# Feed-forwards and output projections with the activations stationary, and a residual stream with tokens on partitions

## The chip, the cores and the metric

The kernel runs on one core of a Trainium2 chip. The metric is the device time of one execution in microseconds, the median over runs. All inputs are float32, the batch is one, and the sequence has 256 tokens. Only weights are packed and constants laid out on the host; the whole computation is one launch.

## The reference

The model is two layers of a decoder trunk, D = 2048. Layer 0 mixes with differential attention and an S5 state-space layer, layer 1 with RWKV-7. Around each mixer and each feed-forward stand two RMS norms, one before and one after:

```python
def _rmsnorm(x, gain, eps=1e-6):
    return x * lax.rsqrt(jnp.mean(x * x, axis=-1, keepdims=True) + eps) * gain

def _swiglu(h, w_gate, w_up, w_down):            # D_FF = 5632
    return (jax.nn.silu(h @ w_gate) * (h @ w_up)) @ w_down

for layer in range(2):
    gains = norm_gains[layer]
    h = _rmsnorm(x, gains[0])
    m = even_mixer(h) if layer == 0 else rwkv7_time_mix(h)   # each ends in "@ w_out" or "@ w_o", 2048 x 2048
    x = x + _rmsnorm(m, gains[1])
    f = _swiglu(_rmsnorm(x, gains[2]), w_gate[layer], w_up[layer], w_down[layer])
    x = x + _rmsnorm(f, gains[3])
```

In layer 1 the normed x of a token is mixed with that of the token before it, with six sets of weights per channel, ahead of the projections (receptances, keys, values, and three low-rank gates).

## The kernel before

**Layout.** Activations lie with channels on partitions: an array of 2048 channels and 256 tokens is sixteen tiles of 128 channels by 256 tokens. A norm's mean over channels is therefore a sum over partitions and tiles. Squares are summed tile by tile on GpSimd (`Acc`, line 464), and products with a column of 1/2048 on TensorE give a mean for each token (`rms_bc`, line 409). The power -1/2 is GpSimd's. Then `spread` (line 434) makes a diagonal of it and multiplies by ones, so that the value of each token stands on all partitions, for use as a tile of 128 by 256.

**Products.** For accuracy each operand is split into a rounded part and the rest, both float32r (`split`, line 390; for weights lines 317 and 318), and a product is three: high by high, high by low, low by high. In `mmb` (line 341) a 128x128 block of weights is stationary and 256 tokens move: three matmuls of 256 columns for each block. `n_outer` (line 351) runs over all k for one output tile of 128 channels; `k_steps` (line 372) holds several output tiles open and steps through k, so that TensorE can start when the first tiles of its input are there. `values` (line 1399) has it the other way already, for the values of both layers: 128 tokens of activations are stationary and four blocks side by side (512 columns) move, three matmuls for each half of the tokens.

**Weights.** All weight blocks lie in one stream in the order of use, eight to a chunk of 512 KB. `block` (line 321) takes the next; every eighth one calls `chunk_load` (line 308): a DMA on SyncE's queue, a rounding cast on ScalarE and a subtraction on VectorE, with three buffers for each of the three tiles, at a high priority.

**Order.** Instructions of an engine are ordered by a planner that simulates the program and takes priorities into account. `strict` keeps TensorE in the order in which the code is written. `warm` (line 295) issues products into a bank that nothing reads, while TensorE waits. PSUM's eight banks are three "pg", two "pa" and three "pb".

**The feed-forward** (`ffn`, line 1036). It first forms R of the mixer's norm. `post` (line 479) gives x += m R tile by tile, while the products of three tiles of gate and three of up follow in `k_steps` as x comes in. Each tile of x is split for the products with its gain as factor; the norm's R over x, which is known only at the end, is applied to the gate and up sums (lines 1070 and 1071). `pair` forms silu(gate) times up and splits it. Then `proj_out` (line 510) gives the down projection, its gain, its squares, and in layer 0 also the sums of x y and y y, so that `rms_two` (line 444) has R of the next layer's norm without a pass over the new x.

**The mixers' ends.** Layer 0's output projection is split: a first part (heads 0 to 4) fills waits of the mixer (`first`, line 744), and the rest is added to it (line 768). In layer 1 `wo` (line 1499) does it in four groups of heads: three of them as filler between the steps of the recurrence (`rwkv_values`), the last one by itself. `rwkv_keys` (line 1147) begins with x += m R0, h = x R1, the mix for the receptances and seven receptance tiles in `k_steps`.

**The end** (`forward`, line 1662): R of the last norm, `post`, and a store for every two tiles.

## Time and profile before

| | |
|---|---|
| median of three runs | 2703.03 us (2702.46 to 2706.29) |
| span of the profiled execution, first to last instruction | 2701.4 us |
| mean granted TensorE clock | 0.975 |
| read from and written to HBM | 448.02 MB, 27.79 MB |

The profiled execution's own time is given as its span alone; the nearest run is 1.1 us above it, the median 1.6.

| stretch, us from the span's start | what runs |
|---|---|
| 0 to 487 | layer 0's mixer, with its output projection at 428 to 487 |
| 487 to 535 | x += m R, first three tiles of gate and up |
| 535 to 1262.6 | feed-forward 0 |
| 1262.6 to 1329 | norm, mix, seven receptance tiles |
| 1329 to 1902 | layer 1's mixer; its last output projection group from 1877 |
| 1902 to 1955 | as at 487 |
| 1955 to 2681.7 | feed-forward 1 |
| 2681.7 to 2701.4 | last norm, sum and store |

A profile line of a group reads: line of the kernel, engine, operation, tile written <- tiles read, shapes, count | busy us, mean ns of one | idle time of the engine before them, and what ended it. A row of busy time by stretches gives the stretch, its length, busy time and instruction count of each engine, the granted clock, and DMA's share and rate. Matmuls are pipelined, so a matmul's own duration (its latency) is longer than the distance to the next; the distance is what a stream costs.

### The profile page before, as it was taken

Reading aid. Unit: us, or ns where it says so; the run is one execution under the profiler, and the core shown is the slowest. Engines: PE = TensorE matmul, PEld = TensorE weight load, DVE = VectorE, ACT = ScalarE, POOL = GpSimd, SP = SyncE. Lnnn points to the kernel's source line nnn. Section 1 sums busy time; section 2 is a strip of 40 time slices with the busy share of each in tenths; the row PEclk is TensorE's granted clock in tenths of the full one; section 3 lists DMA queues with packets and bytes.
Section 4 is the critical chain, followed back from the end, with each engine's and each line's share of the span. In section 5 each row is a group of like instructions: output and inputs, shape, how many; then the busy total and the mean of one; then the engine's idle time right before and its main releaser. Section 6 shows DMA issues by size and latency. Waiting matters only on the chain. (4 is left out here: it accounts for less than half of the span.)

```text
span 2701.4 us, 51244 instructions
## 1 busy us (share of the span) xinstructions
PE 2584.4 (96%) x20736; PEld 2459.2 (91%) x20736; DVE 1762.8 (65%) x2736; ACT 1180.7 (44%) x1847; POOL 585.0 (22%) x818
## 2 busy tenths in 40 slices
PE   8898899999999999998999889899899999999997
PEld 7775679899999999998899878799899999999997
DVE  7978875765556554445769979587766565554444
ACT  5332245544444444433766634353544444444342
POOL 4765622500000001113306530111600000000001
PEclk9999899999999999999999989899999999999999
DMA  6322235555555555555567687764455555555554
GB/s 218 110 102 86 86 125 181 175 186 184 183 183 185 181 191 199 193 181 186 171 209 239 208 220 207 179 198 158 173 187 185 181 187 180 186 181 184 183 182 162
DMA packets 218300, 479.14 MB, mean 177 GB/s; under 512 B 78672, under 2 KB 107600, under 8 KB 217040
## 3 DMA queue, kind: packets, MB, share of 16 engines
q1 hardware_dynamic: 218064, 475.88, 53.3%
q8 instruction: 162, 2.65, 0.4%
q14 instruction: 74, 0.61, 0.1%
HBM read 448.02 MB, written 27.79 MB: 176 GB/s over the span
## 5 line engine op out<-in xcount | busy, mean ns | idle before, releaser
L318 DVE TENSOR_TENSOR wl<-wr,wh 128x1024 fp32r<-128x1024 f32 x760 | 956.1, 1259 | 671.1 <-ACT wh L317 669.3
L317 ACT CAST wh<-wr 128x1024 fp32r<-128x1024 f32 x768 | 803.4, 1047 | 1156.1 <-PE pg L293 944.6
L293 PE MATMUL pg<-Z,wh 128*128 128x256 f32 x6368 | 1170.9, 286 | 18.5 <-ACT wh L317 11.0
L293 PEld LDWEIGHTS pg<-Z,wh 128*128 128x128 f32 x6368 | 1001.5, 194 | 39.7 <-issue 20.4
L293 PE MATMUL pg<-Z,wl 128*128 128x256 f32 x3184 | 905.5, 285 | 4.9 <-DVE wl L318 4.9
L293 PEld LDWEIGHTS pg<-Z,wl 128*128 128x128 f32 x3184 | 615.8, 194 | 6.5 <-DVE wl L318 6.4
L293 PE MATMUL pg<-PP,wh 128*128 128x256 f32 x2304 | 416.2, 283 | 0.0
L293 PEld LDWEIGHTS pg<-PP,wh 128*128 128x128 f32 x2304 | 359.4, 192 | 0.0
L293 PE MATMUL pg<-PP,wl 128*128 128x256 f32 x1152 | 326.0, 283 | 0.0
L293 PE MATMUL pg<-MX,wh 128*128 128x256 f32 x1408 | 271.4, 292 | 7.6 <-DVE MX L400 3.7
L475 POOL TENSOR_TENSOR n<-n,n 128x256 f32<-128x256 f32 x84 | 92.3, 1099 | 770.2 <-ACT n L473 768.3
L293 PEld LDWEIGHTS pg<-MX,wh 128*128 128x128 f32 x1408 | 224.7, 196 | 9.8 <-DVE MX L400 4.2
L293 PEld LDWEIGHTS pg<-PP,wl 128*128 128x128 f32 x1152 | 221.2, 192 | 0.0
L293 PE MATMUL pg<-MX,wl 128*128 128x256 f32 x704 | 201.7, 292 | 6.4 <-DVE wl L318 6.4
L293 PEld LDWEIGHTS pg<-MX,wl 128*128 128x128 f32 x704 | 136.9, 197 | 7.9 <-DVE wl L318 7.9
L544 POOL TENSOR_TENSOR ac<-f,M 128x256 f32<-128x256 f32 x1 | 0.7, 746 | 487.7 <-DVE M L542 487.7
L293 PE MATMUL pg<-X,wh 128*128 128x256 f32 x512 | 93.5, 283 | 0.0
L293 PE MATMUL pg<-wh,MX 128*128 128x512 f32 x256 | 90.0, 413 | 2.9 <-issue 2.6
L293 PEld LDWEIGHTS pg<-X,wh 128*128 128x128 f32 x512 | 79.9, 192 | 0.0
L293 PE MATMUL pg<-X,wl 128*128 128x256 f32 x256 | 72.4, 283 | 0.0
L1071 DVE TENSOR_TENSOR f<-pg,n 128x256 f32<-128x256 f32 x84 | 35.7, 425 | 52.2 <-PE pg L293 52.2
L293 PEld LDWEIGHTS pg<-wh,MX 128*128 128x128 f32 x256 | 49.7, 194 | 13.8 <-issue 3.0
(379 smaller groups left out, 3222.6 us busy)
## 6 DMA issues: line engine op xcount, KB each, us to landing
wr<-wst SPq DMA_DIRECT2D x776, 512.0 KB, 3.6
dr<-H SPq DMA_DIRECT2D x16, 512.0 KB, 4.2
CH<-dr SPq DMA_DIRECT2D x16, 512.0 KB, 4.7
dr<-X SPq DMA_DIRECT2D x12, 512.0 KB, 3.4
X<-dr SPq DMA_DIRECT2D x6, 1024.0 KB, 7.1
dr<-ak SPq DMA_DIRECT2D x16, 256.0 KB, 3.8
ln<-lnb SPq DMA_DIRECT2D x8, 512.0 KB, 4.4
S<-s5bc SPq DMA_DIRECT2D x4, 512.0 KB, 6.5
```

Source lines behind the costliest of these rows:

```text
L293: self.pe(self.nc.tensor.matmul(out, lhsT, rhs, start=start, stop=stop))
L317: nc.scalar.copy(h, r)
L318: (nc.gpsimd if pool else nc.vector).tensor_tensor(l, r, h.bitcast(F32), op=ALU.subtract)
L475: nc.gpsimd.tensor_tensor(self.cur[0], self.cur[0], sq, op=ALU.add)
L544: (v if last else gp).tensor_tensor(s[:, 1], xt, m[n], op=ALU.mult)
L1071: v.tensor_tensor(ur, u, Rh, op=ALU.mult)
```

## The change

Gate, up, down and both output projections take the form of `values`: 128 tokens stationary, 512 columns of weights moving. Their results, and x, m and the norms' sums, then have tokens on partitions: two arrays of 128 tokens by 2048 channels. R is a column per token half, used as a scalar for each partition; gains become rows that are loaded from DRAM. What goes into the next product must have channels on partitions, and is turned by transposes on TensorE (`flip`). The helpers `rms_bc`, `spread` and `Acc` stay in use for the first norm only; `post`, `proj_out` and `store_x` are gone.

The core of it (comments that the diff takes out, and lines of the same kind, are left out):

```diff
+    def rms(self, ss, eps=1e-6):
+        v = self.nc.vector
+        s, ms, r = (self.tmp("ts", [P, 1]) for _ in range(3))
+        v.tensor_reduce(s, ss, axis=mybir.AxisListType.X, op=ALU.add)
+        v.tensor_scalar(ms, s, 1.0 / DM, eps, op0=ALU.mult, op1=ALU.add)
+        self.nc.gpsimd.tensor_tensor(r, ms, self.mhalf[:, 0:1], op=ALU.pow)
+        return r, ms
...
+    def gain_row(self, l, j, c, n=512):
+        t = self.tmp("gr", [P, n])
+        o = (3 * l + j - 1) * DM + c
+        self.nc.sync.dma_start(t, self.d["cr"][:, o:o + n])
+        return t
+
+    def wmm(self, ps, zh, zl, W, t, start, stop):
+        ts, (h, l) = slice(t * P, t * P + P), W
+        self.mm(ps, zh[:, ts], h, start, False)
+        self.mm(ps, zh[:, ts], l, False, False)
+        self.mm(ps, zl[:, ts], h, False, stop)
+
+    def wide(self, w, n, zH, zL, ks, pss, nb=4, late=0, hook=None, first=True, last=True):
+        ks, held = list(ks), []
+        o = [ps[:, :nb * P] for ps in pss]
+        for a, k in enumerate(ks):
+            W = self.blocks(w, k, n, nb)
+            f, e = first and a == 0, last and a == len(ks) - 1
+            if a >= len(ks) - late:
+                held.append((k, W, f, e))
+                continue
+            for t in range(2):
+                self.wmm(o[t], zH[k], zL[k], W, t, f, e)
+                yield nb / 2
+            if hook and a == TR:
+                hook()
+        for t in range(2):
+            for k, W, f, e in held:
+                self.wmm(o[t], zH[k], zL[k], W, t, f, e)
+                yield nb / 2
...
+    class Out:
+        def add(self, pss, c, n=512, part=None, last=False):
...
+            g, cs = p.gain_row(self.l, self.j, c, n), slice(c, c + n)
+            for t in range(2):
...
+                if self.xs is not None:
+                    xt = p.tmp("xt", [P, n])
+                    nc.sync.dma_start(xt, self.xs[t][:, cs])
+                with p.hi():
+                    if part is not None:
+                        v.tensor_tensor(m, ps, part[t][:, cs], op=ALU.add)
+                        ps = m
+                    nc.scalar.activation(junk(), ps, AF.Square, accum_out=ss[:, 0])
+                    (gp if part is not None and not last else v).tensor_tensor(m, ps, g, op=ALU.mult)
+                    if xt is not None:
+                        (v if last else gp).tensor_tensor(xt, xt, m, op=ALU.mult)
+                        nc.scalar.activation(junk(), m, AF.Square, accum_out=ss[:, 2])
+                        nc.scalar.activation(junk(), xt, AF.Copy, scale=2.0, accum_out=ss[:, 1])
...
+    def flip(self, ps, src):
+        for i in range(src.shape[1] // P):
+            self.pe(self.nc.tensor.transpose(ps[:, i * P:(i + 1) * P], src[:, i * P:(i + 1) * P], self.ident))
...
     def ffn(self, x, l, macc):
+            def stage(t, k, n, g, eng):
+                cs = slice(k * P, (k + n) * P)
+                xp, xg = x[t][:, cs], m[t][:, cs]
+                with self.hi():
+                    v.scalar_tensor_tensor(xp, xg, R0[t], xp, op0=ALU.mult, op1=ALU.add)
+                    eng.tensor_tensor(xg, xp, g, op=ALU.mult)
+                    ps = self.pa()
+                    self.flip(ps, xg)
+                    pv = ps[:, :n * P].rearrange("p (a b) -> p a b", b=P)
+                    self.split(self.half(sH, k, n, t), self.half(sL, k, n, t), pv)
...
+            pss = [[self.pg(), self.pb()] for _ in range(3)]
+            grp = [(gw, 0), (uw, 0), (gw, 4)]
+            for t in range(2):
+                for k, n in ((0, 1), (1, 3)):
+                    stage(t, k, n, g[:, k * P:(k + n) * P], v)
+                if t == 0:
+                    held = [self.blocks(gw, k, 0) for k in range(4)]
+                for k in range(4):
+                    self.wmm(pss[0][t], zH[k], zL[k], held[k], t, k == 0, False)
+            for q in range(4):
+                for i, (w, c) in enumerate(grp):
+                    if i and q < 3:
...
+                        stage(i - 1, 4 * q + 4, 4, g, gp)
+                    if q or i:
+                        self.run(self.wide(w, c, zH, zL, range(4 * q, 4 * q + 4), pss[i], first=q == 0, last=q == 3))
...
+            def pair(i, g, u):
+                for t in range(2):
+                    with self.hi():
+                        a, b = self.tmp("e", [P, 512]), self.tmp("e", [P, 512])
+                        nc.scalar.activation(a, g[t], AF.Tanh, scale=Rh[t])
+                        v.scalar_tensor_tensor(a, a, 1.0, g[t], op0=ALU.add, op1=ALU.mult)
+                        nc.scalar.activation(b, u[t], AF.Copy, scale=Rh[t])
+                        v.scalar_tensor_tensor(a, a, R[t], b, op0=ALU.mult, op1=ALU.mult)
+                    todo.append((s, t, a))
+
+            def flips():
+                while todo:
+                    s, t, a = todo.pop(0)
+                    with self.hi():
+                        ps = self.pa()
+                        self.flip(ps, a)
+                        ts = slice(t * P, t * P + P)
+                        self.split(s[:, 0:4, ts], s[:, 4:8, ts], ps.rearrange("p (a b) -> p a b", b=P))
...
+            for n in range(NW):
+                o, e = [self.pg(), self.pb()], n == NW - 1
+                ks = list(range(36, KF)) + list(range(36)) if e else range(KF)
+                self.run(self.wide(dw, 4 * n, pH, pL, ks, o, late=LATE if e else 0, hook=flips))
+                out.add(o, n * 512, last=e)
+            x = self.load_x([a[:] for a in xs])
+            self.warm(W3 if l else W2)
...
     def rwkv_keys(...):
-        for k, xk in post:
-            with self.tc.high_priority(offset=HP if k in HK else 0):
-                (gp if k in HG else v).tensor_tensor(h[k], xk, R, op=ALU.mult)
-                mix(0, rr, k)
-            rs = next(steps)
+        for q in range(4):
+            cs = slice(q * 512, q * 512 + 512)
+            for t in range(2):
+                with self.hi():
+                    v.scalar_tensor_tensor(x[t][:, cs], m[t][:, cs], R0[t], x[t][:, cs], op0=ALU.mult, op1=ALU.add)
+                    v.tensor_scalar(m[t][:, cs], x[t][:, cs], R1[t], None, op0=ALU.mult)
+                    ps = self.pb()
+                    self.flip(ps, m[t][:, cs])
+                    nc.scalar.copy(self.half(hs, 4 * q, 4, t), ps.rearrange("p (a b) -> p a b", b=P))
+            for k in range(4 * q, 4 * q + 4):
+                with self.hi():
+                    mix(0, rr, k)
+                rs = next(steps)
+        for t in range(2):
+            nc.sync.dma_start(xs[t][:], x[t])
...
+    def wo(self, oT, g, part, out=None):
+        zH, zL = ({g * GP + p: oT[g][:, a + p] for p in range(GP)} for a in (0, GP))
+        for n in range(NW):
+            pss, cs = [self.pg(), self.pg()], slice(n * 512, n * 512 + 512)
+            yield from self.wide("wo", 4 * n, zH, zL, range(g * GP, g * GP + GP), pss, late=LATE)
...
     def forward(self, out):
+        for t in range(2):
+            for k, n in ((0, 4), (4, 4), (8, 4), (12, 4)):
+                cs = slice(k * P, (k + n) * P)
+                v.scalar_tensor_tensor(x[t][:, cs], m[t][:, cs], R[t], x[t][:, cs], op0=ALU.mult, op1=ALU.add)
+                ps = self.pa()
+                self.flip(ps, x[t][:, cs])
+                nc.scalar.copy(m[t][:, cs], ps)
+                nc.sync.dma_start(out[:, k:k + n, t * P:(t + 1) * P], m[t][:, cs].rearrange("p (a b) -> p a b", b=P))
```

TR is 6, NW 4, LATE 4, W1 to W3 20. `blocks` takes n blocks side by side out of one chunk, and `half` names four tiles' columns of one token half. `rms_two` has the same terms as before, on columns. In layer 0 the first part of the output projection is done 512, 512, 512, 256 and 256 columns wide, over five k each, and the rest with [pg, pg] and the last of four with `late=4`; W1 warm-up products follow it.

More of the change, by code (lines that the diff above doesn't have):

```diff
@@ L760, in main @@
                         self.split(gH[m], gL[m], o, 0.5)
-                yield from first(range(O2, KD))
+                yield from first(14, 2)
                 yield from until(lambda: st["att"] == 8)
-                st["m"], acc = self.arr_m(), Prog.Acc(self)
-                m = st["m"]
-                for n in range(KD):
-                    ps = yield from self.tile("out", n, mH + gH, mL + gL, range(OH, 16))
-                    with self.hi():
-                        v.tensor_tensor(m[n], ps, part[n], op=ALU.add)
-                        acc.add(m[n], n == KD - 1)
-                        nc.scalar.activation(m[n], m[n], AF.Copy, scale=self.gain(0, 1, n))
-                st["acc"] = acc
+                out = Prog.Out(self, self.halves([self.mslots() for _ in range(2)]), 0, 1)
+                for n in range(NW):
+                    pss = [self.pg(), self.pg()]
+                    e = n == NW - 1
+                    yield from self.wide("out", 4 * n, mH + gH, mL + gL, range(OH, 16), pss, late=LATE if e else 0)
+                    out.add(pss, n * 512, part=part, last=e)
+                st["out"] = out
             sides = [[0, att()], [L0, s5()]]
@@ L1432, in rwkv_values @@
                     gp.memset(t[64 * h:64 * h + 64, :, 1 - h], 0.0)
-        tl = [self.xslots(), self.mslots()]
-        part = [tl[n // 8][:, n % 8] for n in range(KD)]
+        part = self.halves([self.xslots(), self.mslots()])
         V = [Vs[:, g % 2] for g in range(NG)]
```

332 lines of the change are left out of this document (145 added, 187 removed), and 2 rows, old and new, of the table TMP.

## The prediction

> **What bounds the kernel now.** I read the page first, for the shares.
>
> ```profile
> span 2701.4 us, 51244 instructions
> PE 2584.4 (96%) x20736; PEld 2459.2 (91%) x20736; DVE 1762.8 (65%) x2736; ACT 1180.7 (44%) x1847; POOL 585.0 (22%) x818
> PEclk9999899999999999999999989899999999999999
> ```
>
> TensorE is busy nearly throughout, every product has a weight load of its own (equal counts), and the clock is near full. The median of the runs, 2703.03, stands 1.6 us above this span; I make the sum against the span and add 1.6 at the end. The chain of waits, in order of time, says whether TensorE is also what time waits for:
>
> ```profile
> 1960.54 721.31 PE pg L293 x6011
> ```
>
> The whole second feed-forward is one piece: product after product, nothing else waited for. So a saving in the time per product there comes off the span in full. Next, the busy time by stretches: both feed-forwards, one run of products that already are 512 columns wide (the values of layer 0), and the places between the stages.
>
> ```profile
> core 0: us, PE busy (x) PEld busy (x) DVE busy (x) ACT busy (x) POOL busy (x), PEclk, DMA share, GB/s
> 42.92:64.56 21.64, 21.64 (x96) 17.91 (x96) 17.59 (x54) 8.63 (x9) 14.21 (x35) 1.00 0.56 195
> 487.07:535.10 48.03, 42.35 (x339) 39.82 (x338) 40.28 (x48) 25.68 (x47) 31.33 (x31) 1.00 0.49 169
> 600.00:1000.00 400.00, 400.00 (x3336) 400.00 (x3334) 237.64 (x312) 166.82 (x209) 0.00 (x0) 1.00 0.54 183
> 1262.57:1277.71 15.14, 11.07 (x92) 8.90 (x90) 11.70 (x25) 4.31 (x10) 8.58 (x16) 1.00 0.37 131
> 1277.71:1329.06 51.35, 44.31 (x336) 43.09 (x337) 48.19 (x83) 36.96 (x79) 24.97 (x71) 0.93 0.50 157
> 1590.00:1622.00 32.00, 21.98 (x339) 18.03 (x339) 12.24 (x23) 9.80 (x16) 4.66 (x11) 0.78 0.95 222
> 1622.00:1905.00 283.00, 267.74 (x2438) 242.47 (x2437) 219.34 (x376) 122.94 (x195) 50.32 (x37) 0.95 0.66 189
> 1901.74:1955.43 53.69, 45.33 (x340) 42.03 (x339) 40.44 (x49) 26.45 (x49) 33.69 (x33) 0.94 0.41 148
> 2000.00:2400.00 400.00, 400.00 (x3336) 400.00 (x3335) 238.34 (x314) 167.03 (x210) 0.00 (x0) 1.00 0.53 183
> 2681.69:2701.40 19.71, 3.55 (x30) 2.69 (x28) 13.19 (x26) 1.13 (x3) 8.39 (x10) 0.71 0.28 106
> ```
>
> In the feed-forwards 3336 products, some three of them begun before the window, take 400 us: 0.1200 us per 256 columns at full clock, in both layers. VectorE is busy for 59% there and ScalarE for 42%, GpSimd idle. The 96 wide products, start to start 95 steps, take 21.64 us: 0.2278 us per 512 columns. Two narrow products cost 0.2400, so each pair made wide saves 0.0122. Both rows read as 0.107 us per 256 columns and 0.013 us per product: the change halves the second part.
>
> [...]
>
> **The stream.** A feed-forward has 44 x 16 blocks each of gate, up and down, three products each: 6,336 narrow products per layer, 3,168 wide ones after. Over both layers 6,336 pairs x 0.0122 = 77.3 us saved. The two output projections (256 blocks each) give 768 pairs, 9.4 us at most. They hold two of three "pg" banks per step and, in layer 1, two weight chunks until the second token half is done, so part may return as waits: I take 7, with 0 and 10 as ends.
>
> The weights must keep up: eight blocks are a chunk, used up in 2.88 us before and 2.73 after.
>
> ```profile
> L318 DVE TENSOR_TENSOR wl<-wr,wh 128x1024 fp32r<-128x1024 f32 x760 | 956.1, 1259 | 671.1 <-ACT wh L317 669.3 <-PE pb L293 1.3 <-ACT s L956 0.2
> L317 ACT CAST wh<-wr 128x1024 fp32r<-128x1024 f32 x768 | 803.4, 1047 | 1156.1 <-PE pg L293 944.6 <-issue 132.8 <-DMA wr<-wst 48.5
> ```
>
> A chunk takes 1.05 us of ScalarE and 1.26 of VectorE, both under 2.73, and the cast waits mostly for TensorE to free a buffer (944.6 us), rarely for the transfer (48.5): supply runs ahead of use. DMA would go from 183 to about 193 GB/s; 1590:1622 shows 222 at a share of 0.95. I cost the supply at nothing; the cover is this lead. Were it gone, TensorE would stay at the 183 GB/s of now and the stream's 77.3 us would be lost.
>
> **Transposes.** Tokens now come out on partitions, so each pair's result is turned back: 11 column groups x 2 token halves x 2 layers = 44 groups of four transposes in the stream. A like group is in the trace:
>
> ```profile
> 1831.67 0.60 PE L1555 MATMUL pa<-cg,CH 128*128 128x128 f32 x4
> 1832.02 0.48 PE L293 MATMUL pg<-MX,wh 128*128 128x256 f32 x2
> 1832.34 0.28 PE L293 MATMUL pg<-MX,wl 128*128 128x256 f32 x1
> ```
>
> The four push the next product back by 0.35 us, and the two after them take 0.32 instead of 0.24: 0.43, so 44 x 0.44 = 19.4 us added. Each feed-forward's entry also turns 32 tiles of x, at 0.11 each 3.5 us, 7.0 together.
>
> **The pair's chain.** Turned tiles are taken on TensorE, whose order is fixed, seven k-steps after the up product ends: 42 x 0.2278 = 9.6 us. The chain that must be done by then is priced by like tiles of 128x512:
>
> ```profile
> L1640 ACT ACTIVATE ft<-Y 128x512 f32<-128x512 f32 x8 | 5.0, 631 | 3.6 <-DVE Y L1639 3.6
> L1584 ACT COPY gs<-pb 128x512 f32<-128x512 f32 x16 | 9.4, 584 | 8.6 <-PE pb L293 8.2
> L1659 DVE TENSOR_TENSOR ft<-pa,G 128x512 f32<-128x512 f32 x8 | 5.5, 688 | 1.3 <-PE pa L1655 1.2
> L1646 DVE TENSOR_TENSOR Y<-Y,ft 128x512 f32<-128x512 f32 x8 | 5.5, 686 | 0.1
> L1636 POOL TENSOR_TENSOR ft<-ft,ln 128x512 f32<-128x512 f32 x8 | 10.6, 1322 | 77.3 <-DMA ln<-lnb 77.3
> L999 ACT ACTIVATION_READ_ACCUMULATOR t<-t,ts 128x1 f32 x32 | 6.0, 187 | 0.0
> ```
>
> VectorE has four operations of 0.69 behind a tanh of 0.63, 3.4 us, and up to 9.6 / 2.73 = 3.5 weight chunks at 1.26 among them: 7.8 us, under 9.6. So the flips wait for nothing. VectorE's whole load falls: before, five operations of 256 per tile; after, six of 512 for four tiles.
>
> **Entries of the feed-forwards.** Before, from the last product of the projection to the 289th of the feed-forward, 48.03 and 53.69 us pass, of which 288 x 0.1200 = 34.6 are products: 13.5 and 19.1 are lost to the sums of squares, the spread of R over partitions and a tile-by-tile start. After, R is a column per token. The first half's twelve held products come ahead of the second's (2.7 us), and its chain of partial sum, square, accumulator and R fits about there: 0.69 + 0.63 + 0.19, three small operations and a power as in these rows:
>
> ```profile
> 489.31 0.15 DVE L421 TENSOR_SCALAR ts<-pb 128x2 f32<-128x2 f32 x1
> 489.54 0.71 POOL L422 TENSOR_TENSOR ts<-ts,mhalf 128x2 f32<-128x2 f32 x1 [2.41 <-DVE ts L421]
> ...
> 1270.88 4.53 PE L300 MATMUL pa<-cg 128*128 128x256 bf16 x40
> ```
>
> That is 2.7 us; the first 128 columns, turned and split, then need some 1 us, and the twenty warm-up products that stand first (4.53 / 40 = 0.11 each) bound the start at 2.2 us. I take 3.5 for the start and 3 for waits at the first two stages, whose gain product is GpSimd's (1.32 us) and whose flips stand ahead of ready products in TensorE's order. Gain 13.5 + 19.1 - 2 x 6.5 = 19.6; ends 10 and 25.
>
> **Into layer 1.** 15.14 us pass from the last down product to the first receptance product, then 51.35 for 336 products that need 40.3, with VectorE busy for 48.19. VectorE's residual work in it:
>
> ```profile
> L490 DVE TENSOR_TENSOR X<-X,n 128x256 f32<-128x256 f32 x16 | 10.1, 647 | 0.0
> ...
> L1180 DVE TENSOR_TENSOR H<-X,m 128x256 f32<-128x256 f32 x7 | 4.9, 717 | 0.0
> ```
>
> After, the chain to R1 is square, gain, product with x, two accumulators, six small operations and two powers, then two operations of 512, four transposes, a copy and the mix: about 10 us. VectorE's residual work falls from 15.0 to 11.0 us (sixteen operations of 0.69 for x and h), ScalarE gains eight copies of 0.58, and 32 transposes (3.5 us) join on TensorE. I take a gain of 8; ends -5 (512 columns of both halves must stand before the first mix) and 13.
>
> **The end.** Before, 19.71 us from the last product. After: square 0.63 + 0.19, three small operations, a power, then the second half's four operations of 0.69 and some two of the first half's that the same queue still holds, transposes 0.44, copy 0.58, and a transfer:
>
> ```profile
> dr<-ak SPq DMA_DIRECT2D x16, 256.0 KB, 3.8
> X<-dr SPq DMA_DIRECT2D x6, 1024.0 KB, 7.1
> ```
>
> 2.0 + 6 x 0.69 + 1.0 + 3.8 = 11.0: gain 8.7; ends 6 and 12. The copy of x now leaves in 1 MB pieces on SyncE's queue, ahead of later chunks; 7.1 us each lies within the lead of the buffers, and I cost it at nothing, with 7 us per feed-forward if the lead is short. The same queue gets 24 gain rows of 256 KB, 6 MB beside the weights' 400, in stretches that the DMA rows show at a share of 0.56 or less; x for the three sums comes in eight pieces of 256 KB, where sixteen of half that came before. Both at nothing, under the same cover. For waits at new places that no row shows I put 5 us; ends 0 and 45 (a us at each of some 45 bank, flip and chunk hand-overs).
>
> **Sum.** 77.3 + 7 - 19.4 - 7.0 + 19.6 + 8 + 8.7 - 5 = 89.2. 2701.4 - 89.2 + 1.6 = 2613.8, say 2614 us.
>
> **Rivals.** *The stream stutters.* Strict order puts flips and bank hand-overs in front of ready products, and held chunks leave one buffer for prefetch. For it: 1622:1905, with small pieces between products, loses 15 us and runs at clock 0.95. Against: 42.92:64.56 stands among the narrow ones without a gap. At 45 us of such waits, 2614 + 40 = 2654. [...] By the 0.95 of that window the 1,440 us of stream would grow by 76, to 2690; the feed-forward rows show 1.00 while cycling three banks, against it. 0.10 for the waits, 0.03 for the clock.
>
> *Width gives nothing.* If a wide product costs 0.2400 in the long stream, or the supply holds it at the old pace, 84 us go: 2698, faster by just under 0.2%. Against: 95 steps of 0.2278. 0.03.
>
> *Slower: the flips wait for the pair.* If ScalarE and VectorE do not overlap, because each queue is in order and chunk casts stand between the steps, the chain is 4 x 0.63 + 4 x 0.69 + 3.5 x (1.05 + 1.26) = 13.4 us or more, and TensorE waits at each of 22 hooks for what exceeds 9.6. From 13.7 us on (4.1 x 22 = 90) the change is a loss; with the splits behind it, at 14.5, the time is 2614 + 108 = 2722. Against: VectorE is idle for 41% of the stream. 0.05.
>
> *More than said:* the entries at their best ends and freer VectorE in layer 1, about 2585: 0.07.
>
> **Numbers.** The forecast has 0.72, between 2590 and 2640. The range 2582 to 2665 takes in most of the better case and of the waits. 0.2% (5.4 us) is what a measurement of this kernel can tell from no change. Faster: 0.72 + 0.10 + 0.03 + 0.07 = 0.92; same: 0.03; slower: 0.05.
>
> **What would show it.** Right: wide products 0.227 to 0.229 apart in both feed-forwards, each about 720 us of products plus 10 of flips; under 8 us from the last projection product to the first gate product; about 11 us after the last product. Wrong: idle time on TensorE ahead of transposes that ends with VectorE (the flips wait), ahead of a first product into a bank (hand-over), waits for wh or wl, a granted clock under 1.00 in the stream, or a longer stretch from down to the receptances.

## The result and the profile after

The changed kernel takes 2645.47 us, the median of four runs (2639.70 to 2648.46), against 2702.93 before (2702.46 to 2706.29): a ratio of 0.9784, with a 95% interval from 0.9770 to 0.9799. 57 us are gained where 89 were forecast. The profiled execution is the 2639.70 one, the lowest of the four; its sum is made against its own span, and it holds 63.5 us of gain.

The page of the changed kernel, the three lines that answer to those of before:

```profile
span 2637.9 us, 36715 instructions
PE 2508.4 (95%) x13816; PEld 2097.0 (79%) x13816; DVE 1643.5 (62%) x2370; ACT 1189.5 (45%) x1752; POOL 444.8 (17%) x694
PEclk9998899999999999998999998999899999999999
```

A third fewer matmuls and weight loads for the same sums, and the busy time of TensorE falls by 76 us. The span falls by less, 63.5 us, so TensorE is idle for some 12 us more than before. The busy time by stretches of the changed kernel (first two columns: the stretch and its length; then the engines' busy times with their counts, the granted clock, and DMA). The first five rows are its stages, cut at the last product of each layer's output projection and of each down projection, the next two lie inside the feed-forwards. Of the last four, the first, second and fourth are the hand-overs into feed-forward 0, into layer 1 and into feed-forward 1; the third runs from layer 1's first product to the step that moves the first receptances out of PSUM:

```profile
core 0: us, PE busy (x) PEld busy (x) DVE busy (x) ACT busy (x) POOL busy (x), PEclk, DMA share, GB/s
0.00:483.92 483.92, 440.65 (x2495) 349.34 (x2496) 371.37 (x762) 186.82 (x354) 243.76 (x405) 0.95 0.40 134
483.92:1232.09 748.17, 738.90 (x3310) 610.38 (x3308) 391.53 (x373) 339.57 (x397) 18.89 (x16) 0.99 0.60 197
1232.09:1877.71 645.62, 583.99 (x4653) 522.35 (x4652) 486.87 (x852) 328.03 (x623) 170.97 (x261) 0.94 0.66 195
1877.71:2625.73 748.02, 737.69 (x3309) 609.61 (x3308) 387.42 (x375) 329.87 (x371) 10.59 (x11) 0.99 0.58 193
2625.73:2637.90 12.17, 7.13 (x54) 5.29 (x52) 6.29 (x11) 5.18 (x10) 0.54 (x1) 1.00 0.58 173
...
600.00:1000.00 400.00, 400.00 (x1803) 332.08 (x1803) 212.22 (x198) 183.54 (x199) 0.00 (x0) 1.00 0.58 190
2000.00:2400.00 400.00, 400.00 (x1803) 331.98 (x1802) 212.30 (x198) 183.53 (x199) 0.00 (x0) 1.00 0.57 190
...
483.92:497.07 13.15, 3.91 (x27) 2.56 (x25) 11.40 (x21) 7.21 (x20) 3.21 (x3) 0.78 0.72 266
1232.09:1251.07 18.98, 4.81 (x30) 3.29 (x28) 15.77 (x36) 7.64 (x20) 3.72 (x19) 0.68 0.45 170
1251.07:1303.21 52.14, 45.40 (x344) 44.78 (x345) 35.22 (x66) 38.24 (x81) 9.05 (x46) 0.89 0.40 126
1877.71:1891.19 13.48, 3.57 (x27) 2.62 (x25) 11.16 (x23) 7.36 (x20) 1.79 (x3) 0.73 0.92 357
```

The stream is as forecast: 400 of 400 us busy at full clock in both layers, nothing waited for, no idle time ahead of a transpose. The 3,168 wide products of a feed-forward stand 0.227 us apart. In the 13.15 us of the entry (and the 13.48 of the second) TensorE has 27 instructions, most of them the twenty warm-up products, and in the 18.98 into layer 1 it has 30. Stage by stage, with the forecast's terms put where they belong (per feed-forward 38.65 for the width, less 9.7 and 3.5 for transposes, plus 7.0 or 12.6 for the entry; the projections by halves; 8 for layer 1's start):

| stretch | before | after | gained | forecast |
|---|---|---|---|---|
| layer 0's mixer, to the last projection product | 486.9 | 483.9 | 3.0 | 3.5 |
| to feed-forward 0's last down product | 775.7 | 748.2 | 27.5 | 32.4 |
| to layer 1's last projection product | 639.2 | 645.6 | -6.4 | 11.5 |
| to feed-forward 1's last down product | 779.8 | 748.0 | 31.8 | 38.1 |
| to the end | 19.8 | 12.2 | 7.6 | 8.7 |

The forecast's 5 us for waits at new places go off its 94.2. So the misses are in the feed-forwards (11) and in layer 1's stage (18). The timeline of the changed kernel at the second entry shows what TensorE waits for (start, duration, engine, line, operation, count; in brackets the idle time before and who ended it; SPq is SyncE's queue, where a line is the issue of a transfer):

```profile
1877.10 0.69 DVE L571 TENSOR_TENSOR M<-M,G 128x512 f32<-128x512 f32 x1 [0.85 <-ACT gs L570]
...
1879.88 2.86 DVE L1098 SCALAR_TENSOR_TENSOR X<-M,ts,X 128x128 f32<-128x128 f32 x5
...
1882.66 1.22 DVE L327 TENSOR_TENSOR wl<-wr,wh 128x1024 fp32r<-128x1024 f32 x1
1882.77 0.33 SPq L1137 DMA_DIRECT2D dr<-X  x1
1883.80 0.68 DVE L571 TENSOR_TENSOR M<-M,G 128x512 f32<-128x512 f32 x1
1883.91 0.33 SPq L321 DMA_DIRECT2D wr<-wst  x1
1884.33 1.72 SPq L511 DMA_DIRECT2D gr<-cr  x2
...
1885.40 2.87 DVE L1098 SCALAR_TENSOR_TENSOR X<-M,ts,X 128x128 f32<-128x128 f32 x5 [0.67 <-POOL ts L459]
...
1889.75 2.52 DVE L1099 TENSOR_TENSOR M<-X,gr 128x128 f32<-128x128 f32 x4 [1.48 <-DMA gr<-cr]
...
1890.19 1.34 PE L592 MATMUL pa<-cg,M 128*128 128x128 f32 x4 [9.89 <-DVE M L1099]
```

Read it from the bottom. The first transposes wait 9.89 us for x times its gain row (L1099), and that waits for the row's load (L511), which is issued only at 1884.33 and lands 5.4 us later. It stands in SyncE's queue behind two others. The copy of the first half of x, 1 MB (L1137), goes at 1882.77, when the last of the five updates of that half is done (L1098, 2.86 us, of which only the first two are wanted yet). The load of a weight chunk (L321) goes at 1883.91, when VectorE's subtraction (L327, 1.22) is done. The row's own packets move only from 1887.7 on, when the copy's are through and most of the chunk's. The first entry is the same: copy at 488.75, chunk at 489.88, row at 490.26, landed 5.0 us later, with 9.2 us of waiting. Why the planner put the row there is not shown. It is not for the second half's product with the projection's gain (L571): the load is issued before that product ends, 1884.33 against 1884.48, and 490.26 against 490.46 at the first entry.

Into layer 1, the same view:

```profile
1235.93 0.69 DVE L573 TENSOR_TENSOR xt<-xt,M 128x512 f32<-128x512 f32 x1
...
1237.07 2.74 DVE L1276 SCALAR_TENSOR_TENSOR X<-M,ts,X 128x512 f32<-128x512 f32 x4 [0.36 <-POOL m L1250]
...
1239.72 0.21 DVE L472 SCALAR_TENSOR_TENSOR ts<-ts,ts 128x1 f32<-128x1 f32 x1
...
1241.11 1.67 DVE L1277 TENSOR_SCALAR M<-X,ts 128x512 f32<-128x512 f32 x4 [0.27 <-POOL ts L475]
...
1243.49 2.07 DVE L1276 SCALAR_TENSOR_TENSOR X<-M,ts,X 128x512 f32<-128x512 f32 x3
1245.48 0.21 DVE L473 SCALAR_TENSOR_TENSOR ts<-ts,ts,ts 128x1 f32<-128x1 f32 x1
...
1251.07 1.01 PE L302 MATMUL pg<-MX,wh 128*128 128x256 f32 x3 [2.70 <-ACT MX L403]
```

The small steps to R1 (L472 to L474, 0.2 us each) stand behind updates of x for all 2048 channels, in both halves, though the first product needs 512 of them. Later TensorE waits once more, before the products of the last 512 channels. The list of TensorE's waits from 1260 to 1310, and the timeline of ScalarE ahead of it:

```profile
PE pg L302 <- ACT MX L403: 6.6, 1, 6.6
```

```profile
1289.41 0.89 ACT L1249 ACTIVATE MX<-H,n 128x255 f32<-128x255 f32 x2
...
1292.34 0.91 ACT L1249 ACTIVATE MX<-H,n 128x255 f32<-128x255 f32 x2
...
1293.14 1.01 ACT L403 CAST MX<-m 128x256 fp32r<-128x256 f32 x3
```

ScalarE makes the gate's mixes (MX<-H), which are wanted later, ahead of the receptances' casts (L403).

**Theory.** The stream's terms hold, and the missing time is in three hand-overs, where the order of the work in the queues and one late load make chains long that are short by their own operations (TensorE waits 9.2 and 9.9 us at the entries; 18.98 us pass into layer 1). **Rivals:** the stream saves less than said; the transposes cost more; the hand-overs are bound by work, or what is won there is waited for again.

### The profile page after: what moved, and what is told of

Read it like the earlier page. It is cut to its first block, busy times and chain, and to the rows that moved or that the text cites. A ratio compares the mean times of both kernels' runs of the same rounds, so it can differ in the third digit from the quotient of the medians.

```text
span 2637.9 us, 36715 instructions
## 1 busy us (share of the span) xinstructions
PE 2508.4 (95%) x13816; PEld 2097.0 (79%) x13816; DVE 1643.5 (62%) x2370; ACT 1189.5 (45%) x1752; POOL 444.8 (17%) x694
## 5 line engine op out<-in xcount | busy, mean ns | idle before, releaser
L327 DVE TENSOR_TENSOR wl<-wr,wh 128x1024 fp32r<-128x1024 f32 x760 | 946.0, 1246 | 790.2 <-ACT wh L326 784.7
L302 PE MATMUL pg<-wh,Z 128*128 128x512 f32 x1664 | 636.8, 394 | 0.5 <-DVE Z L409 0.4
L302 PE MATMUL pb<-wh,Z 128*128 128x512 f32 x1408 | 547.2, 389 | 0.1
L302 PEld LDWEIGHTS pg<-wh,Z 128*128 128x128 f32 x1664 | 314.0, 189 | 71.2 <-issue 4.9
L302 PE MATMUL pg<-wl,Z 128*128 128x512 f32 x832 | 325.2, 391 | 0.0
L302 PEld LDWEIGHTS pb<-wh,Z 128*128 128x128 f32 x1408 | 264.2, 188 | 55.7 <-ACT Z L403 0.5
L302 PE MATMUL pb<-wl,Z 128*128 128x512 f32 x704 | 273.9, 389 | 0.0
L302 PE MATMUL pg<-wh,PP 128*128 128x512 f32 x576 | 223.3, 389 | 0.0
L302 PE MATMUL pb<-wh,PP 128*128 128x512 f32 x576 | 223.1, 389 | 0.0
L302 PE MATMUL pg<-Z,wh 128*128 128x256 f32 x736 | 151.5, 306 | 16.2 <-ACT wh L326 10.5
L302 PEld LDWEIGHTS pb<-wl,Z 128*128 128x128 f32 x704 | 132.2, 188 | 27.5
L302 PEld LDWEIGHTS pg<-Z,wh 128*128 128x128 f32 x736 | 122.0, 205 | 36.4 <-issue 19.7
```

What stands on the lines that cost most here:

```text
L302: self.pe(self.nc.tensor.matmul(out, lhsT, rhs, start=start, stop=stop))
L327: (nc.gpsimd if pool else nc.vector).tensor_tensor(l, r, h.bitcast(F32), op=ALU.subtract)
```

## The experiments

All twelve runs were timed beside the kernel before. Durations of stages are from one profiled execution each; "feed-forwards" is from the last projection product to the last down product, layer 0's and layer 1's. "The changed kernel" is the one above.

### The stream: each wide product as two narrow ones

```diff
     def wmm(self, ps, zh, zl, W, t, start, stop):
-        self.mm(ps, zh[:, ts], h, start, False)
...
+        w = c // 2 if self.order[-1][0].rstrip("01") in ('gate', 'up', 'down') else c
+        for i in range(0, c, w):
+            b = slice(i, i + w)
+            self.mm(ps[:, b], zh[:, ts], h[:, b], start and i == 0, False)
...
```

> Each product of the feed-forwards with 512 weight columns moving is issued as two with 256 moving, same stationary block, same PSUM bank, same sums; all else as in the changed kernel. Theory (the width is worth 12.2 ns for each pair of products of 256 columns): 6,336 pairs by 0.0122 is 77 us more, 2645 + 77 = 2722, with steps of 0.120 us between products. Rival (the width is worth nothing, the gain came from the other edits): within 5 us of 2645. Rival (reloading the stationary block is dearer, since there the activations change in each product): 2735 or more.

2724.54 us (2718.64 to 2725.78), ratio to before 1.0076 [1.0058, 1.0095]: a little slower than before. The stretches of the two feed-forwards, and one inside:

```profile
492.63:1280.49 787.86, 778.19 (x6477) 776.25 (x6476) 391.25 (x374) 338.35 (x398) 18.90 (x16) 0.99 0.58 188
1921.90:2710.87 788.97, 777.80 (x6478) 776.27 (x6476) 387.03 (x376) 328.32 (x371) 10.60 (x11) 0.99 0.57 184
...
600.00:1000.00 400.00, 400.00 (x3343) 400.00 (x3342) 202.17 (x190) 173.37 (x190) 0.00 (x0) 1.00 0.56 180
```

They are 39.7 and 41.0 us longer than 748.2 and 748.0, 80.7 in all, 0.0127 us for each of 6,336 pairs. The rate in the stream is that of before again (3343 in 400 us with the transposes among them; 3336 before). So without the width the rest of the change is a loss of some 21 us, and the width is worth what the forecast said.

### The transposes: each group issued twice

```diff
                         self.flip(ps, a)
+                        self.flip(ps, a)
```

> Each group of four transposes of a feed-forward's products is issued twice into the same PSUM tile; all else as in the changed kernel. Theory (44 groups at 0.44 us, nothing hidden, no wait before them): 19.4 us more, 2665, each feed-forward 9.7 us longer (758). Rival (their price is the wait for the operand or for PSUM, not the transposes): under 8 us more. Rival (they upset the stream behind them): 30 us more or over.

```profile
488.84:1246.78 757.94, 748.35 (x3397) 619.91 (x3396) 392.61 (x373) 339.83 (x397) 18.93 (x16) 0.99 0.60 194
1884.45:2642.91 758.46, 748.00 (x3398) 619.88 (x3396) 387.94 (x375) 330.32 (x371) 10.61 (x11) 0.99 0.59 191
```

The feed-forwards are 9.7 and 10.5 us longer: 20.2 for 44 groups, 0.46 each where 0.44 was forecast. They are paid for in full and wait for nothing. The median, 2657.05 (2649.94 to 2661.56), is only 11.6 above the changed kernel's; the other 9 come back in layer 1's recurrence, which was not edited (below).

### The entries: the gain row loaded early, then also the order

In the first kernel the row for the first 512 columns is loaded early, at the kernel's start for layer 0 and ahead of layer 1's mixer for layer 1, into two of the five "n" buffers; the first columns are taken as 256 and 256 in place of 128 and 384. In the second, the updates of x for the later columns also stand behind the first columns' gain products on VectorE.

```diff
-            g = self.gain_row(l, 2, 0)
...
-                for k, n in ((0, 1), (1, 3)):
-                    stage(t, k, n, g[:, k * P:(k + n) * P], v)
+                for k, n in ((0, 2), (2, 2)):
+                    stage(t, k, n, self.row0[k // 2], v)
...
# the second kernel, in stage():
+                with self.hi(), self.tc.issue_after(first_xg[-1].ins) if k >= 4 else nullcontext():
```

> Each feed-forward's first 512 gain columns are loaded at the kernel's start (layer 1: before the layer 1 mixer) into two tiles of their own, so that the entry waits for no load; the first pieces of each half are two of 256 columns in place of 128 and 384. Theory (the entries start late because the gain row is fetched late): from the last projection product to the first gate product 6.5 to 8.5 us in place of 13.2 and 13.5, the time 10 to 13 us under the changed kernel's 2645, so 2632 to 2635; the x-updates still stand ahead of the second half's gain product, so a wait of up to 3 us before the second half's first flip shows up. Rival (the chain from the last product over R to the flip is long by itself, and the row is only the last of several): 11 to 12 us to the first product, 2640 to 2643. Rival (the missing time isn't at the entries): within 2 us of 2645.

> As the kernel with the early gain row, and VectorE's updates of x behind the first 512 columns are issued after the first 512 columns' gain products of both halves. Theory (VectorE's queue order delays the second half's R): first gate product 6 to 7.5 us after the last projection product, and before the second half's first flip under 1 us of wait, so another 2 to 5 us for both entries together: 2628 to 2632. Rival (the updates moved behind are then late for the later columns): the wait reappears before the flips of columns 512 to 2047, and the time is that of the kernel with the early row or more.

Both missed: 2649.28 us (2646.41 to 2649.96) and 2650.88 (2648.60 to 2651.48). The first gate product did come 7.7 and 8.4 us after the last projection product in the first, 5.7 and 6.4 in the second, and the first's feed-forwards were 744.1 and 744.9. Two things ate it. In both, the planner's order in layer 0 came out another, and its mixer took 497.8 and 499.8 us where ten profiles with that order unchanged have 483.5 to 495.4. (Whether the load did it, or the two buffers that layer 0's first norm also uses, no run separates.) The same 25 us of the changed kernel and of the first experiment:

```profile
25.00:50.00 25.00, 24.94 (x177) 23.50 (x178) 22.43 (x78) 9.07 (x10) 2.08 (x5) 1.00 0.61 196
```

```profile
25.00:50.00 25.00, 20.02 (x142) 19.50 (x141) 20.11 (x67) 8.76 (x12) 5.64 (x9) 0.86 0.47 153
```

And in the second, VectorE ran the updates moved behind in one go, ahead of a split that TensorE wanted: 3.5 us of waiting at each entry, so that the feed-forwards came out at 746.5 and 748.1. That was its rival.

```profile
510.61 5.10 DVE L1099 SCALAR_TENSOR_TENSOR X<-M,ts,X 128x512 f32<-128x512 f32 x3
...
515.63 0.74 DVE L409 TENSOR_TENSOR Z<-pa,Z 128x256 fp32r<-128x256 f32 x2
```

### The entries without the row, and without moving anything else

The next two need no row: x itself is transposed for the first 512 columns, and the gain is a factor for each partition in the split. The first does only that. The second also orders the queues: each later update of x behind the split of the columns before it, and ScalarE's squares behind the splits.

```diff
-                    eng.tensor_tensor(xg, xp, g, op=ALU.mult)
+                    if k >= 4:
+                        eng.tensor_tensor(xg, xp, g, op=ALU.mult)
                     ps = self.pa()
-                    self.flip(ps, xg)
+                    self.flip(ps, xg if k >= 4 else xp)
...
+                    for i in range(0 if k >= 4 else n):
+                        ts = slice(t * P, t * P + P)
+                        self.split(zH[k + i][:, ts], zL[k + i][:, ts], pv[:, i], self.gain(l, 2, k + i))
...
# the second kernel also:
+                with self.hi(), self.tc.issue_after(before[k // 4].ins) if k >= 4 else nullcontext():
+                    x_ins = v.scalar_tensor_tensor(xp, xg, R0[t], xp, op0=ALU.mult, op1=ALU.add)
...
+                with self.tc.issue_after(self.hi_ins.ins):
                     nc.scalar.activation(self.tmp("j", [P, 512]), x[t][:, q * 512:(q + 1) * 512], AF.Square,
```

> Of the two edits at the entries only one: the first 512 columns of x are transposed themselves and the gain is a scale for each partition afterwards; the order of the queues is left to itself. Theory (two causes, the late row and the order, of about equal weight): first gate product 5 to 9 us after the last projection product, feed-forwards of 743 to 746 us, between the 748 of the changed kernel and the 741 of the kernel with both edits. Rival (the late row alone was the cause): 741 to 742. Rival (the order alone): 747 or more.

> Only the two entries differ from the changed kernel, and the queues of layer 0 and of layer 1's mixer keep their order: for the first 512 columns x itself is transposed and the gain is applied afterwards as a scale for each partition, so that no gain row is waited for, and the later updates of x on VectorE and the squares on ScalarE stand behind the first columns' steps of both halves and then each behind the columns before. Theory (the entries are long because of the late gain row and of VectorE's order): first gate product 5.5 to 7.5 us after the last projection product in place of 13.1 and 13.5, and from the last projection product to the last down product 740 to 743 us in place of 748.2 and 748.0, since here the later columns are not late; the time 2632 to 2637 where the changed kernel has 2645. Rival (what is won at the start is waited for again within the next 20 us, as with the early row, where the two feed-forwards won 4.1 and 3.1 us of 5.4 and 5.0): feed-forwards of 744 or more, 2640 to 2648.

Without the row alone, the first gate product comes after 3.2 and 3.5 us (sooner than expected) and the feed-forwards take 743.3 and 744.2. With the order as well, the start is the same, and:

```profile
486.62:1227.60 740.98, 736.89 (x3309) 608.44 (x3308) 392.89 (x373) 340.54 (x401) 21.47 (x16) 1.00 0.61 198
1876.91:2618.17 741.26, 737.13 (x3309) 608.46 (x3308) 388.27 (x375) 331.02 (x375) 13.14 (x11) 1.00 0.60 195
```

The two causes are both there: 4.8 and 3.9 us are the row's, 2.4 and 2.9 the order's. The start of 3.2 and 3.5 is the 3.5 that the forecast took for it. Of the 9.9 us by which the first product comes sooner without the row, that kernel keeps half or less; the rest is waited for in the next columns.

The clock has a part in both. In the changed kernel the trace has it at half for 10.2 us at each entry, until 4.5 and 3.0 us after the first gate product, and products there stand 0.43 us apart and more, in place of 0.227. Without the row it is at half for 3.4 and 6.8 us, behind a wait of 3.6 us between two products. With the order as well no two products of the entry are more than 1.7 us apart, and the clock stays full; the row up to the first gate product of layer 0 is:

```profile
486.60:489.83 3.23, 2.97 (x26) 2.29 (x25) 3.17 (x6) 2.27 (x5) 1.63 (x1) 1.00 0.28 77
```

So the shares of the row and of the order hold what the clock gives back; no run takes it apart. The second kernel takes 2633.56 us (2629.47 to 2637.06), ratio 0.9739 [0.9725, 0.9754], 11.9 under the changed one, as its two feed-forwards say (13.9). The first takes 2631.93 (2622.86 to 2636.07), no more than the second although its feed-forwards are 5.3 longer; that again is the recurrence (below).

### Layer 1's start: the order on VectorE, then on ScalarE too

```diff
-                with self.hi():
+                with self.hi(), self.tc.issue_after(last.ins) if q else nullcontext():
                     v.scalar_tensor_tensor(x[t][:, cs], m[t][:, cs], R0[t], x[t][:, cs], op0=ALU.mult, op1=ALU.add)
...
+                with self.tc.issue_after(last.ins):
                     mix1(j, k, H[k], k in MP[n])
# the second kernel: the updates behind the first 512 columns' mixes alone, and the gate's mixes
+                e = ends[min(k // 4 + 2, 3)]
+                with self.tc.issue_after(e[0].ins), self.tc.issue_after(e[1].ins):
                     mix1(j, k, H[k], k in MP[n])
```

> The entries stay as in the changed kernel; at the start of layer 1's mixer VectorE's updates of x for each 512 columns are issued behind the mixes of the 512 before, and the gate's mixes behind the receptances' mixes. Theory (order in VectorE's queue, not work, makes the hand-over long): last down product to first receptance product 13 to 15 us in place of 19.0, no gap of 6.6 us before the last 512 columns' products, receptances done 8 to 12 us sooner; of that 5 to 11 us reach the end, so 2634 to 2640. Rival (the chain is bound by work or by the cross-engine steps): first product still at 17 us or later, within 2 us of 2645. Rival (what is won is waited for again at the recurrence): receptances sooner by 8 us or more, the last output projection product of layer 1 sooner by under 3 us.

The first product came at 14.1 us, as expected, but the receptances were evacuated from 75.4 us on, later than the 71.1 of the changed kernel; 2648.32 us (2646.39 to 2653.82). Its timeline in the last 512 columns:

```profile
1279.33 5.69 ACT L1249 ACTIVATE MX<-H,n 128x255 f32<-128x255 f32 x14
...
1285.22 4.10 ACT L1249 ACTIVATE MX<-H,n 128x255 f32<-128x255 f32 x10
...
1285.69 1.41 DVE L1276 SCALAR_TENSOR_TENSOR X<-M,ts,X 128x512 f32<-128x512 f32 x2
```

The gate's mixes on VectorE were held back, but their first step is ScalarE's, and there 24 of them now ran ahead of the receptances' steps; and each update of x had to wait for the mixes of the columns before. My theory had named one queue of two. The second kernel orders both and frees the updates:

> Only layer 1's start differs from the changed kernel: updates of x for columns 512 to 2047 stand on VectorE behind the first 512 columns' mixes, and the gate's mixes stand on VectorE and on ScalarE behind the receptances' mixes of two column groups later. Theory (order in both queues makes this stage long): first receptance product at 14 us after the last down product as in the run before, no gap over 2 us until the receptances' end, receptances evacuated from 61 to 65 us on in place of 71.1, and the gates' first step at 150 to 155 us in place of 160.4. Rival (the gap only moves to the gate's products, whose mixes are then late): receptances sooner, the gates' first step at 158 us or later. For the end: between 3 and 10 us by the theory, under 3 by the rival; one run of the mixers differs from the next by some 5 us, so the stage marks decide.

First product at 14.1 us, receptances evacuated from 60.7 us on (71.1), the gates' first step (here always the first operation of line 1378 of the changed kernel) at 148.9 (160.4): 11.5 us sooner, and the gap does not move to the gate's products. The median, 2641.94 us (2630.51 to 2644.95), shows only 3.5 of it and is inconclusive by itself; its profile has the longest of the ten mixers of layer 0 (495.4).

### Both together

> The edits of the two kernels before together: entries with the gain applied after the transposes and ordered queues, and layer 1's start with ordered queues. Theory (the hand-overs hold the time that the forecast missed, and they add up): 2645 less 10 to 16 for the entries and 3 to 10 for layer 1's start, 2619 to 2632. Rival (hand-overs shortened are paid for by later waits): 2638 or more.

2622.21 us (2617.57 to 2627.23), ratio to before 0.9698 [0.9683, 0.9714]: the fastest of all, 23.3 us under the changed kernel. The same edit of layer 1's start that showed 3.5 us by itself gives 11.3 on top of the ordered entries (2633.56 to 2622.21), what its marks had said. Its span, and the three stages from layer 0's mixer on:

```profile
span 2620.7 us, 36707 instructions
```

```profile
489.84:1230.84 741.00, 736.92 (x3309) 608.62 (x3308) 392.60 (x373) 339.75 (x401) 21.49 (x16) 1.00 0.62 198
1230.84:1866.76 635.92, 583.61 (x4653) 521.02 (x4652) 487.88 (x851) 327.46 (x623) 170.57 (x261) 0.95 0.67 197
1866.76:2608.01 741.25, 737.14 (x3309) 608.63 (x3308) 388.17 (x375) 330.20 (x375) 13.13 (x11) 1.00 0.60 195
```

TensorE's busy time in them is that of the changed kernel within 2 us; only the idle time is gone.

### The smaller terms, and the changed kernel again

```diff
# narrow products in the output projections: as above, with
+        w = c // 2 if self.order[-1][0].rstrip("01") in ('out', 'wo') else c
# nothing held back
-LATE = 4
+LATE = 0
```

> Each wide product of the two output projections is issued as two of 256 columns, same stationary block and sums; the feed-forwards as in the changed kernel. Theory (768 pairs at 0.0122 us, 9.4 at most, 7 by the forecast since part is waited for): the last column groups of both projections take 2 to 2.5 us longer each than in the changed kernel, the whole 5 to 9 us. Rival (the projections are held by their hand-overs, not by products): under 1 us for each group. The median can't tell them apart if the mixers vary by 5 us; the stretch of the groups can.

The last 264 wide products of layer 0's projection take 60.21 us in the changed kernel, the same work in 528 narrow ones 62.81: 2.6 us. The last group of layer 1, 96 wide products, takes 23.36 (22.24 in its second run) against 22.92 narrow: within 0.7 us either way. Both wide runs hold a wait of 0.5 us, and the 23.36 also has five steps of 0.43 us, at half the clock. So the theory holds in layer 0 and the rival in layer 1. The median, 2651.14 (2645.71 to 2653.53), can't be used: layer 0's order changed as well, and its mixer took 498.1.

> No products are held back at the end of the projections and of the down products: both token halves end together. Theory (the twelve held products, 2.7 us, let the first half's norm run under the second half's products): each of the two entries and the end 1.5 to 2.7 us longer, the hand-over to layer 1 too, 6 to 11 us in all, 2651 to 2656. Rival (both halves' steps stand in one queue, so the head start is lost there): within 1 us at each place.

First gate product after 13.7 and 11.8 us (13.1 and 13.5 with held products), feed-forwards of 748.4 and 746.8, layer 1's first product at 18.8, the end 13.2 (12.2): within 1.7 us everywhere, longer only at the first entry (0.6) and the end (1.1). So the theory falls. The rival, which said within 1 us, is nearer; that the head start is lost in the queue is its explanation, and is not shown by itself. The median is 2634.33 (2633.32 to 2637.14) all the same, 11 lower; by the profile the difference is in layer 1 after the gates' first step, 475.1 us where the changed kernel has 485.2 and 489.3.

> The changed kernel once more, nothing edited. Theory (the feed-forwards run at a steady clock, the mixers do not): feed-forwards within 1 us of 748.2 and 748.0 again, while layer 0's mixer takes anything from 484 to 496 us and layer 1's stage 637 to 650, at the same order of instructions. Rival (stages repeat within 1 us): 483.9 and 645.6 again.

2644.71 us (2644.06 to 2653.64), feed-forwards 748.2 and 749.0; layer 0's mixer 491.9 and layer 1's stage 650.6, where the first profile had 483.9 and 645.6. The mixers vary, the feed-forwards do not.

Some kernels have totals that their edited stages do not explain. The difference lies between the gates' first step and the last projection product of layer 1, and it goes with the order in which SyncE's queue has the transfers of that stretch (some 220 beside the weight chunks, issued by the same lines in all kernels); most of what differs is around the second inversion:

| order on SyncE | us, one profile each |
|---|---|
| as in the changed kernel, but for two transfers at most | 485.2 and 489.3 (changed kernel), 489.4 (early row), 485.8 (layer 1's start, first kernel), 480.2 (narrow feed-forwards), 488.3 (gain in the split, and order) |
| another, alike but for six at most | 478.8 (row and order), 476.6 (transposes twice), 475.9 (gain in the split), 479.2 (narrow projections), 475.1 (none held) |

The means are 486.4 and 477.1. No edit was aimed at that order; it came out of the planner one way or the other. The kernels with layer 1's start ordered on both engines, alone and with the entries, have orders of their own and 489.9 and 486.3; the kernel before has one more and 485.5. No run changes this order alone, so that it is the cause of the 9 us is argued from eleven profiles, not shown. The clock is a rival. In these stretches it is at half for 51 to 61 us in five profiles of the first row and for 34 to 41 in all five of the second; the sixth of the first row, with the narrow feed-forwards, has 41 and, with the first order, only 480.2 us. TensorE is busy for 40.2 us of that time on average in the first row and for 27.9 in the second; at half speed that would be some 6 of the 9 us, an estimate. Whether the order makes the difference in the clock, no run tells.

## Why the forecast was right, and where it was wrong

The measured 2645 lies in the stated range, but above 2590 to 2640, where the forecast had put 0.72, and the gain is 57 of 89 us. By number the nearest rival is the stuttering stream, at 2654, and its waits in the stream did not come about. That the range took in the real misses, which lie in the hand-overs, was in part luck: its upper end had been laid for other waits.

**The width** was right: 77.3 us forecast, 80.7 by the experiment, with 0.227 us from product to product. For each pair that is 12.2 ns forecast and 12.7 measured. The **supply** of weights cost nothing, as said: no wait for a chunk in either stream.

**The transposes** were right: 19.4 us forecast for the groups in the stream, 20.2 measured. **The pair's chain** stays under the seven k-steps, no transpose waits in the stream, and so the rival on the slower side did not come about; nor did the stuttering stream, nor the lower clock: 1.00 in both 400 us windows, with TensorE busy for 400 of 400 us.

**The output projections** were somewhat less than the 7 us: 2.6 us for 264 of the 768 pairs, under 1 us in layer 1's last group. The rest is not resolved in mixers that vary by more.

**The entries** were wrong, by 14 us. The feed-forwards gained 59.3 us in all; less 80.7 for the width and plus 20.2 for the transposes, that leaves -1.2 for the entries, where 19.6 - 7.0 = 12.6 was forecast. With the two causes gone the feed-forwards take 741 us in place of 748, and the 12.6 is there (12.8 by the same sum). The step that failed is "I take 3.5 for the start and 3 for waits", and behind it "Both at nothing, under the same cover" for the gain rows. The 3.5 was the right size for the chain, as the experiments got 3.2 and 3.5. What I left out is that the row's load shares SyncE's queue with the copy of x, whose 1 MB I had also costed "at nothing". The copy can only be issued when the last update of its half of x is done; the row is issued behind it, 6.3 and 6.6 us after the last projection product, and its data move behind the copy's and a chunk's. The lead of the buffers covers the weights, but not the first row. The trace shows this order; no run moves the row ahead of the copy and nothing else. And I counted for VectorE the operations that the chain needs, not those that are ready at the same time and go ahead of it.

**Into layer 1** was wrong, by some 15 us at the gates' first step: 153.7 us before, 145.7 forecast, 160.4 measured, 148.9 with the queues in order. The step is "about 10 us" for the chain: it takes 14.1 with the order mended, so 4 us are its own size, and 4.9 are the updates of x in VectorE's queue. The other 6.6 are the wait before the last 512 columns, on ScalarE, where the forecast had seen only the load of eight more copies. For the bad end of that term's range I had one reason (512 columns of both halves), but not this one. VectorE's work did fall, from 48.19 us to 35.2 in the stretch to the receptances, and this bought nothing: the stage was not bound by work.

**The recurrence** behind it had no term. In the changed kernel it got, by the planner's chance, an order of transfers with which it takes some 9 us longer on average than with the other. Why kernels with the same stage marks differ by that much stays open between the order and the clock that goes with it.

**The end** was right: 12.2 us where 11.0 were forecast. **New waits**, 5 us, were right in kind only: none in the stream, all in the hand-overs. The fastest kernel, with both hand-overs mended, is at 2622, 8 us from the forecast of 2614; together with the other order of transfers it was not tried.

## What to carry to other kernels

When an edit shortens a chain, write down for each queue on it what else becomes ready at that moment. At layer 1's start work that was ready early and wanted late went first on two engines: the updates of x on VectorE, 4.9 us, and the gate's mixes on ScalarE, 6.6 us; with both queues in order the gates' first step came 11.5 us sooner. A load that looked covered was not, where it stood in a queue behind a transfer that waited for the chain itself: the gain row was issued 6.3 and 6.6 us after the last projection product, behind a copy of 1 MB, and its part of the two entries was 4.8 and 3.9 us. So look at what is issued ahead of a load, what that waits for, and how many bytes it moves. And judge such edits by the marks of a steady stage, not by the total: here the feed-forwards repeat within 1 us, while the mixers vary by 5 (layer 1, the same kernel twice) to 12 (layer 0) and reorder themselves when something far away is edited.

## What was not expected of the hardware

Layer 0's mixer took 483.5 to 495.4 us in ten profiles with the same order of instructions, and the length goes with the clock that was granted there. Its stretch in the changed kernel stands above (483.92 us, clock 0.95); in the kernel with layer 1's start edited it is:

```profile
0.00:495.40 495.40, 451.51 (x2496) 357.65 (x2496) 373.07 (x762) 186.78 (x354) 240.65 (x405) 0.93 0.40 131
```

TensorE is busy for 91% of it in both, where the feed-forwards, at 99%, have 0.99 or 1.00 in every row above. The trace has the clock at full or at half, nothing between. It is at half for 47.8 us in the two shortest of these mixers (483.5 and 483.9), with TensorE busy for some 40 us of it, and for 71.7 in the two longest (492.6 and 495.4), with some 64; 24 us more of work at half speed is 12 us, an estimate that is as large as the difference. At the entries a gap of 9.2 and 9.9 us in TensorE's work cost more than its own length: the products behind it stood 0.43 us apart and more in place of 0.227, with the clock at half until 4.5 and 3.0 us after the first gate product. Whether gaps make the difference between these mixers, or the clock makes the gaps, no run separates.
